# HGRN2 scores in 32-column tiles with compact copies, and two kinds of copy moved to ScalarE

## The chip, the cores and the metric

The kernel runs on one core of a Trainium2 chip. The metric is device time in microseconds (us) of one execution. The engines of the core are TensorE (PE in the profile, its weight loads PEld), VectorE (DVE), ScalarE (ACT), GpSimd (POOL) and SyncE (SP, which issues DMAs here). Each works through a queue of its own in order.

## The reference, cut to what matters

One decoder layer over 1024 positions: a projection of the normalised input, three groups of heads (HGRN2, a dilated window attention, RWKV-7), an output projection, a gated feed-forward part with a short convolution, a gated embedding and a last norm. The change is in the first two groups of heads. For one HGRN2 head, with 128 key and 128 value dimensions, f in (0, 1) and k = 1 - f:

```python
S_t = diag(f_t) S_{t-1} + (1 - f_t) i_t^T
o_t = S_t^T q_t
scores[i, j] = sum_k q[i, k] * (1 - f[j, k]) * prod(f[j+1 .. i, k])     # j <= i, in a chunk
o = scores @ i + (q * prod(f)) @ state
```

The attention computes, for four heads of 64 dimensions, softmax probabilities of a query block over its near and strided far keys, and multiplies them with the values.

## The kernel before, in words

The layer is a sequence of phases. The projections and RWKV-7 come first; the stretch that the change touches is the second part of the mixing phase (`phase_mix`), about 403 to 570 us in the profile; then come the output projection, the feed-forward part (Winograd-like products, lines L1523 and L1845) and the embedding gate. In the stretch of the change four streams of Python generators are taken in turn by `interleave`: A is HGRN2 head 0 and then head 2, B is head 1 and then head 3, C is the attention (`swa`), F is the rest of the input projection (`project_late`, tiles zp). The Tile framework schedules each engine's queue from this order, so a stream's wait delays the others that are queued behind it on the same engine.

**An HGRN2 head** (`hgrn_head`) holds its vectors with the key dimension on the partitions and 1024 positions along the free dimension, as two halves of 512 with four chunks of 128 positions each; one of the halves is stored in reversed order. Its tiles are f (zl), q (zl), the keys k (hk), the decayed queries qt, the scores S (hS, two halves `S3[0]`, `S3[1]`) and the products of f over growing blocks (hT). It first makes f and the keys 1 - f on VectorE (L1094) and qt = q * f (L1096). Then it makes the scores of each position with itself, two groups of four products 128x128x128 (L1112), and copies the diagonal out of PSUM with `copy_predicated` under a mask (L1114). Then come seven levels l with block size n = 2^(l-1) (1 to 64). A level has the keys of every second block in a compact order (ks, a ScalarE copy at L1123), multiplies them with the queries of the neighbouring block (four products 128x128x128, L1138), updates the keys (GpSimd or VectorE, L1140) and the queries (VectorE, L1142) for the next level, and copies from the 128x512 result those scores that the mask of the level marks (L1145). At level l only pairs of positions in neighbouring blocks of n are kept, so at n up to 16 all kept scores lie in 32x32 blocks on the diagonal of a chunk. After level 7, `triangles` moves one triangle into the other half (L1127). The rest of the head transposes values and keys, forms states and outputs (L1163 to L1237). A level's products wait for the queries of the level before (VectorE) and for ks (ScalarE), which waits for hk.

**The attention** makes, for each of eight query blocks of two head pairs, scores (tiles swq; far keys in products with 64 rows and 32 columns of the array, near keys with 64 rows and 128 columns), probabilities (lg), and in `swa_turn` transposes them (swt) and copies them from PSUM to SBUF (pT): for one head of the pair by ScalarE, for the other by VectorE (L1361). The values product reads pT later (swo).

`group` issues a list of products so that they stand together in TensorE's queue. All PSUM tiles of these streams but swq come from one pool of four banks (tag mx).

Of the kernel before, what the change touches and what calls it, by code (L numbers as in the profile page):

```python
# [10 lines left out]
F32 = mybir.dt.float32  # L11
F32R = mybir.dt.float32r
U8 = mybir.dt.uint8
AF = mybir.ActivationFunctionType
ALU = mybir.AluOpType
# [3 lines left out]
P = 128  # L19
T = 1024  # L20
HT = 512
# [16 lines left out]
CC_ID, CC_BONE, CC_MSK, CC_Q, CC_HG, CC_RU = 0, 128, 256, 512, 640, 640 + 9 * 128  # L38
NC0 = 640
# [3 lines left out]
def shape_constants():  # L43
    c = np.zeros((P, NCC), np.float32)
    pp = np.arange(P)[:, None]
    ff = np.arange(P)[None, :]
    c[:, CC_ID:CC_ID + P] = pp == ff
    same = (pp // 64) == (ff // 64)
    c[:, CC_BONE:CC_BONE + P] = same
    c[:, CC_MSK:CC_MSK + P] = same & (pp < ff)  # L50
    c[:, CC_MSK + P:CC_MSK + 2 * P] = same & (pp <= ff)
    c[:, CC_HG:CC_HG + P] = pp == ff
    for l in range(7):
        n = 1 << l
        c[:, CC_HG + (l + 1) * P:CC_HG + (l + 2) * P] = (pp // n) ^ 1 == ff // n
    c[:, CC_HG + 8 * P:CC_HG + 9 * P] = pp < ff
    c[:, CC_Q:CC_Q + P] = pp // 32 == ff // 32
    c[:, CC_RU:CC_RU + P] = same & (ff % 64 >= 32) & (pp % 64 < 32)
    qi, qr = pp % 32, pp // 32
    near = P + 4 * qi + qr - np.arange(2 * P)[None, :]  # L60

    def far(ds):
        return np.concatenate([P * d + 4 * (qi - np.arange(32)[None, :]) for d in ds], axis=1)

    d = np.concatenate([far((6, 5, 4, 3, 2)), np.full((P, 32), -1), near, far((7, 6, 5, 4, 3, 2)), near], axis=1)
    cnt = ((d >= 0) & (d <= 128)).astype(np.float64)
    cnt += (d >= 0) & (d <= 512) & (d % 4 == 0)
    cnt += (d >= 0) & (d <= 2048) & (d % 16 == 0)
    sw = np.where(cnt > 0, 8.0 * np.log(np.maximum(cnt, 1.0)), -1e30).astype(np.float32)
    return c, sw  # L70
# [14 lines left out]
class Trunk:  # L85
# [212 lines left out]
    def hgmask(self, l):  # L298
        o = CC_HG - NC0 + l * P
        return self.cmask[:, o:o + P]  # L300


    def proj(self, j, hooks={}):
# [777 lines left out]
    def hgrn_head(self, h):  # L1081
        nc, mxp, par, spool = self.nc, self.mxp, self.par, self.spool
        j0 = 8 + 4 * h

        def view(t, off, *dims):
            return bass.AP(t.tensor, t.offset + off, [t.ap[0], *dims])

        f = self.zload(j0, self.slot)
        q = self.zload(j0 + 1, self.slot)
        yield  # L1090
        nc.vector.tensor_scalar(f, f, self.olb[:, h:h + 1], self.lb[:, h:h + 1], ALU.mult, ALU.add)
        k = self.slot("hk")
        for a, b in ((0, HT), (HT, 0)):
            nc.vector.tensor_scalar(k[:, a:a + HT], f[:, b:b + HT], -1.0, 1.0, ALU.mult, ALU.add)  # L1094
        qt = self.slot("qt")
        nc.vector.tensor_tensor(qt, q, f, ALU.mult)  # L1096
        yield
# [3 lines left out]
        S3 = [S[:, a:a + HT].rearrange("p (c i) -> p c i", i=P) for a in (0, HT)]  # L1101

        def mask(l):
            return self.hgmask(l).unsqueeze(1).broadcast_to([P, 4, P])

        Tt = self.slot("hT")
        off = 0
        Tc = f
        for i in (0, 1):
            sc = mxp.tile([P, 4, P], F32, tag="mx", name=self.nm("hsc"))  # L1110
            for c in range(4):
                nc.tensor.matmul(sc[:, c, :], k[:, (1 - i) * HT + c * P:(1 - i) * HT + (c + 1) * P],  # L1112
                                 q[:, i * HT + c * P:i * HT + (c + 1) * P], start=True, stop=True)
            nc.vector.copy_predicated(S3[i], mask(0), sc)  # L1114

        def blocks(l):
            n = 1 << (l - 1)
            return n, HT // n, ([HT + n, 2], [2 * n, 256 // n], [1, n])

        def keys(l):  # L1120
            n, nb, half = blocks(l)
            ks = spool.tile([P, HT], F32, tag="sqt", name=self.nm("ks"), bufs=2)
            nc.scalar.copy(view(ks, 0, [n, 2], [2 * n, nb // 2], [1, n]), view(k, 0, *half))  # L1123
            return ks

        def triangles():
            nc.vector.copy_predicated(S3[1], mask(8), S3[0])  # L1127
            nc.gpsimd.affine_select(S3[0], S3[0], [[0, 4], [-1, P]], base=0, channel_multiplier=1, compare_op=ALU.is_ge, fill=0.0)

        last = h == 3  # L1130
        ks = keys(1)
        yield
        for l in range(1, 8):
            n, nb, half = blocks(l)
            qq = view(qt, 0, *half)
            sc = mxp.tile([P, 4, P], F32, tag="mx", name=self.nm("hsc"))
            for c in range(4):
                nc.tensor.matmul(sc[:, c, :], ks[:, c * P:(c + 1) * P],  # L1138
                                 view(qt, c * P, [2 * n, 64 // n], [HT + n, 2], [1, n]), start=True, stop=True)
            (nc.gpsimd if l % 2 else nc.vector).tensor_tensor(  # L1140
                view(k, 0, *half), view(k, 0, *half), view(Tc, nb + 1, [-nb - 1, 2], [2, nb // 2], [0, n]), ALU.mult)
            nc.vector.tensor_tensor(qq, qq, view(Tc, 1, [nb - 1, 2], [2, nb // 2], [0, n]), ALU.mult)  # L1142
            if l < 7:
                ks = keys(l + 1)
            nc.vector.copy_predicated(S3[0], mask(l), sc)  # L1145
            Tn = Tt[:, off:off + nb]
            T3 = Tc.rearrange("p (b two) -> p b two", two=2)
            nc.vector.tensor_tensor(Tn, T3[:, :, 0], T3[:, :, 1], ALU.mult)
            Tc = Tn
            off += nb  # L1150
            if l == 7:
                vc = self.zload(j0 + 2, self.slot)
                if last:
                    triangles()
            yield
        if not last:
            triangles()

        V = self.slot("hV")
        for hf in (0, 1):  # L1160
            pt = mxp.tile([P, HT], F32, tag="mx", name=self.nm("vt"))
# [4 lines left out]
        for hf in (0, 1):  # L1166
            pt = mxp.tile([P, HT], F32, tag="mx", name=self.nm("vt"))
# [10 lines left out]
        for hf in (0, 1):  # L1178
# [6 lines left out]
            for c in range(4):  # L1185
# [3 lines left out]
                dst = st[:, (cc + 1) * P:(cc + 2) * P]  # L1189
# [7 lines left out]
        o, sq = self.slot("ho"), kt  # L1197
# [152 lines left out]
    def swa_turn(self, sp, d, qb, den, lgs):  # L1350
        nc, w = self.nc, 64 * (qb // 2)
        if qb % 2 == 0:
            d["pT"] = [sp.tile([P, 2, HT], F32, tag="pT", name=self.nm("pT"), bufs=3) for _ in lgs]
        else:
            self.uid += 2
        cols = [w + b * P for b in range(2 if qb else 1)] + [b * P for b in range((w + 64) // P)]
        for lg, t, copy in zip(lgs, d["pT"], (nc.scalar.copy, nc.vector.tensor_copy)):
            pt = self.mxp.tile([P, HT], F32, tag="mx", name=self.nm("swt"))
            for i, c in enumerate(cols):
                nc.tensor.transpose(pt[:, i * P:(i + 1) * P], lg[:, c:c + P], self.ident)  # L1360
            copy(t[:, qb % 2, :len(cols) * P], pt[:, :len(cols) * P])  # L1361
        return qb, den, d["pT"]

    def swa_values(self, sp, d, q0, den, pT):
# [698 lines left out]
def lay_out(inp):  # L2063
    f = {k: np.asarray(v) for k, v in inp.items()}

    def cols(v):
        return v.reshape(-1, P).T

    lora = np.concatenate([f["rwkv_w2"][0], f["rwkv_a2"][0]], axis=0)
    par = np.concatenate(  # L2070
        [cols(f["norm_mix_g"][0]), cols(f["norm_ffn_g"][0]), cols(f["norm_ple_g"][0]), cols(f["final_norm_g"]),
         cols(f["hgrn_lower_bounds"][0]), cols(f["hgrn_gnorm_g"][0]), cols(f["rwkv_mu"][0]),
         cols(f["rwkv_w0"][0]), cols(f["rwkv_a0"][0]), cols(f["rwkv_k_k"][0]), cols(f["rwkv_k_a"][0]),
         cols(f["rwkv_r_k"][0].reshape(-1)), cols(f["rwkv_ln_w"][0]), cols(f["rwkv_ln_b"][0]),
         cols(f["ffn_conv_w"][0].reshape(-1)), cols(f["ffn_conv_b"][0]), lora, f["rwkv_g2"][0]], axis=1)
    cst, swm = shape_constants()
    return {
        "xT": np.ascontiguousarray(f["x"][0].T).reshape(ND, P, T),
        "pT": np.ascontiguousarray(f["p"][0, 0].T).reshape(2, P, T),
        "w_in": col_blocks(f["w_in"][0], in_blocks()),  # L2080
        "w_out": col_blocks(f["w_out"][0], range(0, 1024, P)),
        "ffn_up": col_blocks(f["ffn_up"][0], range(0, 5632, P)),
        "ffn_down": np.ascontiguousarray(f["ffn_down"][0]).reshape(NFF, P, 1024),
        "ple_gate": col_blocks(f["ple_gate"][0], range(0, 1024, P)),
        "ple_proj": np.ascontiguousarray(f["ple_proj"][0]).reshape(2, P, 1024),
        "par": np.ascontiguousarray(par),
        "cst": cst,
        "swm": swm,
    }
# [17 lines left out]
```

## Time and profile before

| | us |
|---|---|
| median of three runs | 1410.86 (1410.41 to 1413.49) |
| the profiled execution's own time | 1411.64 |
| its span, first to last instruction | 1409.9 |
| TensorE busy | 1391.4 (99%) |
| VectorE busy | 1082.1 (77%) |
| ScalarE busy | 635.2 (45%) |
| GpSimd busy | 447.2 (32%) |

In the groups of the profile a row reads: line, engine, operation, out<-in by the program's names, the part of the array in use (rows*columns) for TensorE, out<-in sizes, number, then busy us, mean ns of one, and the engine's idle time just ahead of them with what ended it. In the timeline a row is a run of like instructions: start, us from the first's start to the last's end, engine, line, operation, number, and in brackets the idle time ahead of it. An fp32 product stands as two matmul instructions (two passes); the 32-bit "fp32r" products with 512 columns (zp, dp, bg, bv) stand as one. Matmuls overlap, so a matmul's own duration is longer than what it adds to TensorE's time; the step from start to start, or from end to end, is that.

### The profile page before, as it was taken

What the parts mean: (1) busy time and instruction counts of PE and PEld (TensorE: products, weight loads), DVE (VectorE), ACT (ScalarE), POOL (GpSimd) and SP (SyncE); (2) the same over time, 40 slices, a digit from 0 to 9 for tenths busy, and PEclk for the clock granted to TensorE, in tenths of its full rate; (3) what the DMA queues carried; (4) which work ended last, traced back from release to release, by engine and by line L of the source; (5) the groups of instructions that cost most, each with busy time, mean ns of one, the idle gap of its engine ahead of it and who ended that gap; (6) DMA issues with size and microseconds to landing.
All of it is one profiled execution on the core that took longest, in us unless ns stands there. A gap on an engine that the chain in (4) does not pass through costs nothing.

```text
span 1409.9 us, 20332 instructions
## 1 busy us (share of the span) xinstructions
PE 1391.4 (99%) x7458; PEld 1155.3 (82%) x7458; DVE 1082.1 (77%) x1671; ACT 635.2 (45%) x1193; POOL 447.2 (32%) x360
## 2 busy tenths in 40 slices
PE   9999999999999989999999999999999999999997
PEld 7888887888878878888888888888888888888886
DVE  7667575684776788457988888898888799777685
ACT  7531453213444666354544344443435444455552
POOL 2322442223432332221345454454543000002353
PEclk9999999999999999999999999999999999999998
DMA  5223022240252321573333232323334963351443
GB/s 214 79 87 116 31 76 60 67 135 31 76 193 66 107 83 46 172 261 135 121 112 111 86 101 98 110 100 112 112 98 137 358 229 103 113 159 53 129 150 133
DMA packets 80020, 167.78 MB, mean 119 GB/s; under 512 B 20081, under 2 KB 22257, under 8 KB 79921
## 3 DMA queue, kind: packets, MB, share of 16 engines
q1 hardware_dynamic: 66144, 145.97, 31.2%
q10 hardware_dynamic: 12832, 16.98, 3.6%
q0 software_dynamic: 944, 3.54, 0.7%
q8 instruction: 59, 0.97, 0.3%
q14 instruction: 41, 0.33, 0.1%
HBM read 120.05 MB, written 46.40 MB: 118 GB/s over the span
## 4 chain that ended last, share of the span: by engine, by line
PE 94%; DVE 3%; ACT 1%; DMA 1%; issue 1%; POOL 1%; SPq 0%; DVEq 0%; ACTq 0%; POOLq 0%
PE bg L1523 17%; PE bv L1523 13%; PE dp L135 9%; PE dp L137 9%; PE dp L139 9%; PE bg L1845 7%; PE bv L1845 7%; PE hsc L1138 2%; PE bv L135 1%; PE bv L139 1%; PE bv L137 1%; PE bg L139 1%; PE bg L137 1%; PE bg L135 1%; PE zp L135 1%; PE zp L139 1%
## 5 line engine op out<-in xcount | busy, mean ns | idle before, releaser
L135 PE MATMUL dp<-xh,whi 128*128 128x512 f32 x544 | 196.9, 407 | 0.8 <-ACT xh L397 0.8
L137 PE MATMUL dp<-xl,whi 128*128 128x512 f32 x544 | 188.3, 391 | 1.1 <-DVE xl L398 1.1
L139 PE MATMUL dp<-xh,wlo 128*128 128x512 f32 x544 | 188.9, 392 | 0.0
L113 POOL TENSOR_TENSOR wlo<-wraw,whi 128x512 fp32r<-128x512 f32 x63 | 89.2, 1420 | 243.1 <-ACT whi L111 239.0
L113 POOL TENSOR_TENSOR wlo<-raw,whi 128x512 fp32r<-128x512 f32 x84 | 135.7, 1634 | 74.1 <-ACT whi L111 74.1
L1523 PE MATMUL bg<-t,whi 128*128 128x512 f32 x352 | 132.4, 389 | 0.0
L111 ACT CAST whi<-wraw 128x512 fp32r<-128x512 f32 x120 | 72.7, 617 | 117.8 <-PE dp L137 74.9
L139 PEld LDWEIGHTS dp<-xh,wlo 128*128 128x128 f32 x544 | 102.1, 188 | 22.0 <-issue 0.5
L135 PEld LDWEIGHTS dp<-xh,whi 128*128 128x128 f32 x544 | 101.3, 188 | 22.4 <-issue 3.0
L137 PEld LDWEIGHTS dp<-xl,whi 128*128 128x128 f32 x544 | 102.4, 188 | 20.9 <-DVE xl L398 1.7
L113 POOL TENSOR_TENSOR wlo<-s,whi 128x512 fp32r<-128x512 f32 x44 | 66.0, 1500 | 161.5 <-ACT whi L111 150.5
L1845 PE MATMUL bg<-t,whi 128*128 128x512 f32 x308 | 94.9, 389 | 0.0
L1845 PE MATMUL bv<-t,whi 128*128 128x512 f32 x308 | 94.9, 389 | 0.0
L111 ACT CAST whi<-s 128x512 fp32r<-128x512 f32 x66 | 39.0, 620 | 123.3 <-PE bg L1523 115.2
L111 ACT CAST whi<-raw 128x512 fp32r<-128x512 f32 x88 | 52.6, 619 | 92.0 <-issue 48.8
L180 POOL TENSOR_TENSOR rst<-rst,mhalf 128x4 f32<-128x4 f32 (+1 forms) x9 | 10.2, 1138 | 219.8 <-DVE rst L178 219.8
L1523 PEld LDWEIGHTS bg<-t,whi 128*128 128x128 f32 x352 | 66.0, 188 | 13.7
L1841 ACT CAST t<-t 128x512 fp32r<-128x512 f32 x77 | 47.8, 622 | 46.6 <-PE bv L1845 28.8
L1845 PEld LDWEIGHTS bv<-t,whi 128*128 128x128 f32 x308 | 57.8, 188 | 12.0
L1845 PEld LDWEIGHTS bg<-t,whi 128*128 128x128 f32 x308 | 57.8, 188 | 11.9
L1523 PE MATMUL bg<-t,wlo 128*128 128x512 f32 x176 | 67.2, 389 | 0.0
L113 DVE TENSOR_TENSOR wlo<-wraw,whi 128x512 fp32r<-128x512 f32 x57 | 43.5, 766 | 30.5 <-ACT whi L111 26.6
(455 smaller groups left out, 3561.9 us busy)
## 6 DMA issues: line engine op xcount, KB each, us to landing
raw<-in_ffn_up_dram SPq DMA_DIRECT2D x44, 512.0 KB, 3.7
wraw<-in_w_in_dram SPq DMA_DIRECT2D x29, 512.0 KB, 3.7
z<-zst SPq DMA_DIRECT2D x18, 512.0 KB, 2.8
gb<-ct SPq DMA_DIRECT2D x33, 256.0 KB, 2.2
t<-gb SPq DMA_DIRECT2D x33, 256.0 KB, 2.8
t<-gt SPq DMA_DIRECT2D x33, 256.0 KB, 2.7
zl<-z SPq DMA_DIRECT2D x16, 512.0 KB, 4.8
wraw<-in_ple_gate_dram SPq DMA_DIRECT2D x16, 512.0 KB, 3.5
```

The costliest lines, as they stand in the source:

```text
L111: nc.scalar.copy(hi, src)
L113: eng.tensor_tensor(lo, src, hi.bitcast(F32), ALU.subtract)
L135: nc.tensor.matmul(ps[hf], wh, xh[hf], start=first, stop=False)
L137: nc.tensor.matmul(ps[hf], wh, xl[hf], start=False, stop=False)
L139: nc.tensor.matmul(ps[hf], wl, xh[hf], start=False, stop=last)
L180: nc.gpsimd.tensor_tensor(r2[:, :n], r[:, :n], self.mhalf[:, :n], ALU.pow)
L1138: nc.tensor.matmul(sc[:, c, :], ks[:, c * P:(c + 1) * P], view(qt, c * P, [2 * n, 64 // n], [HT + n, 2], [1, n]), start=True, stop=True)
L1523: nc.tensor.matmul(ps, w[part == 2][:, s], X[k][part == 1], start=start and k == part == 0, stop=k == 3 and part == 2, skip_group_check=no ...
L1841: nc.scalar.copy(xh, x)
L1845: nc.tensor.matmul(ps[m], wt[part == 2][:, m * P:(m + 1) * P], (xh, xl)[part == 1], start=k == part == 0, stop=k == NK - 1 and part == 2)
```

## The change

1. The scores of a position with itself and of levels 1 to 6 (n up to 32) are made in products of 32 key columns and 32 queries, those of level 7 in products of 32 key columns and 64 queries. A product (chunk c, block b) writes partitions 32b to 32b+31 of the result. A group has 16 products (32 for the first, which now holds both halves in one PSUM tile), all with the full 128 rows and 32 columns of the array. They are issued through `group`.
2. The result of a group is 128x128 (128x256 for the first and for level 7). For levels 1 to 5 a `copy_predicated` of 128x128 gathers them in a new SBUF tile D (hD, first filled by a plain copy). At level 6, D and the level's result are spread into S by two `copy_predicated` of 128x512 (`place`), at level 7 one; one more puts the second half's diagonal in place.
3. The keys 1 - f are made by ScalarE (activation Copy with scale and bias) instead of VectorE.
4. All transposed probabilities pT are copied by ScalarE.
5. The constant masks are laid out anew to match, in the same space and with the same loads.

```diff
@@ hgrn_head
         for a, b in ((0, HT), (HT, 0)):
-            nc.vector.tensor_scalar(k[:, a:a + HT], f[:, b:b + HT], -1.0, 1.0, ALU.mult, ALU.add)
+            nc.scalar.activation(k[:, a:a + HT], f[:, b:b + HT], AF.Copy, scale=-1.0, bias=1.0)
...
+        def place(i, l, src):
+            w = src.shape[2]
+            dst, m = (t.rearrange("p c (b i) -> p c b i", i=w) for t in (S3[i], mask(l)))
+            nc.vector.copy_predicated(dst, m, src.unsqueeze(2).broadcast_to([P, 4, P // w, w]))
+
+        blocks32 = [(c, b, c * P + 32 * b) for c in range(4) for b in range(4)]
+        D = self.sp.tile([P, 4, 32], F32, tag="hD", name=self.nm("hD"), bufs=2)
...
-        for i in (0, 1):
-            sc = mxp.tile([P, 4, P], F32, tag="mx", name=self.nm("hsc"))
-            for c in range(4):
-                nc.tensor.matmul(sc[:, c, :], k[:, (1 - i) * HT + c * P:(1 - i) * HT + (c + 1) * P],
-                                 q[:, i * HT + c * P:i * HT + (c + 1) * P], start=True, stop=True)
-            nc.vector.copy_predicated(S3[i], mask(0), sc)
+        sc = mxp.tile([P, 2, 4, 32], F32, tag="mx", name=self.nm("hsc"))
+        self.group([(sc[32 * b:32 * b + 32, i, c], k[:, (1 - i) * HT + o:(1 - i) * HT + o + 32], q[:, i * HT + o:i * HT + o + 32])
+                    for i in (0, 1) for c, b, o in blocks32])
+        nc.vector.tensor_copy(D, sc[:, 0])
+        place(1, 0, sc[:, 1])
...
-            sc = mxp.tile([P, 4, P], F32, tag="mx", name=self.nm("hsc"))
-            for c in range(4):
-                nc.tensor.matmul(sc[:, c, :], ks[:, c * P:(c + 1) * P],
-                                 view(qt, c * P, [2 * n, 64 // n], [HT + n, 2], [1, n]), start=True, stop=True)
+            sc = mxp.tile([P, 4, max(32, n)], F32, tag="mx", name=self.nm("hsc"))
+
+            def queries(b, o):
+                if n < 32:
+                    return view(qt, o, [2 * n, 16 // n], [HT + n, 2], [1, n])
+                e = 32 * b // n ^ 1
+                return view(qt, o - 32 * b + e // 2 * 2 * n + e % 2 * (HT + n), [1, n])
+
+            self.group([(sc[32 * b:32 * b + 32, c], ks[:, o:o + 32], queries(b, o)) for c, b, o in blocks32])
...
-            nc.vector.copy_predicated(S3[0], mask(l), sc)
+            if l < 6:
+                nc.vector.copy_predicated(D, self.hgnear(l), sc)
+            else:
+                place(0, l - 4, sc)
+            if l == 6:
+                place(0, 1, D)
@@ swa_turn
-        for lg, t, copy in zip(lgs, d["pT"], (nc.scalar.copy, nc.vector.tensor_copy)):
+        for lg, t in zip(lgs, d["pT"]):
...
-            copy(t[:, qb % 2, :len(cols) * P], pt[:, :len(cols) * P])
+            nc.scalar.copy(t[:, qb % 2, :len(cols) * P], pt[:, :len(cols) * P])
```

The queues as built show how the instructions move. SyncE's queue is the same; GpSimd's has the same operations. On TensorE, levels 4 and 5 of head 1 stand between outputs of head 0 (hpo), the attention's transposes (swt) and the projection (zp). Before:

```order
L1217 MATMUL hpo_4364<-hst_4237,qt_3742 128x128
L1138 MATMUL hsc_4373<-qt_3996,ks_4261 128x128 x4
L1360 MATMUL swt_4384<-cst,lg_4305 128x128 x4
L1360 MATMUL swt_4390<-cst,lg_4308 128x128 x4
L1138 MATMUL hsc_4408<-qt_3996,ks_4380 128x128 x4
L135 MATMUL zp_4431<-xh_105,whi_4421 128x512
```

and now:

```order
L1238 MATMUL hpo_4533<-hst_4394,qt_3742 128x128
L1340 MATMUL hsc_4542<-qt_4080,ks_4430 32x32 x16
L1381 MATMUL swt_4565<-cst,lg_4474 128x128 x4
L1381 MATMUL swt_4571<-cst,lg_4477 128x128 x4
L1340 MATMUL hsc_4589<-qt_4080,ks_4561 32x32 x16
L136 MATMUL zp_4624<-xh_105,whi_4614 128x512
```

Nothing has moved there but the products themselves: 16 small ones where 4 full ones stood, with full-array products on both sides (a size is partitions x columns of the result). Counted over the whole queue, products that follow one with another part of the array (rows*columns) in use number 96 before and 137 now.

On VectorE, where head 2 is at its levels 4 and 5 and head 3 begins (xl belongs to the output of head 1), there stood:

```order
L1142 TENSOR_TENSOR qt_4577<-qt_4577,hT_4609 128x2x32x8
L1145 COPY_PREDICATED hS_4607<-cmask,hsc_4870 128x512
L1237 SCALAR_TENSOR_TENSOR zl_4807<-vt_4881,par,zl_4807 128x512
L1237 SCALAR_TENSOR_TENSOR zl_4807<-vt_4887,par,zl_4807 128x512
L1094 TENSOR_SCALAR hk_4941<-zl_4897 128x512
L1361 COPY pT_4859<-swt_4924 128x384
L162 TENSOR_TENSOR xl_4660<-zl_4807,xh_4659 128x512
L1142 TENSOR_TENSOR qt_4577<-qt_4577,hT_4609 128x2x16x16
L1145 COPY_PREDICATED hS_4607<-cmask,hsc_4929 128x512
```

and now:

```order
L1158 TENSOR_TENSOR qt_4795<-qt_4795,hT_4828 128x2x32x8
L1162 COPY_PREDICATED hD_4827<-cmask,hsc_5148 128x128
L1258 SCALAR_TENSOR_TENSOR zl_5073<-vt_5171,par,zl_5073 128x512
L1364 ISA lg_5206,sden_5191<-swq_5192,swmask 128x384
L1364 ISA sden_5191 128x1
L1258 SCALAR_TENSOR_TENSOR zl_5073<-vt_5177,par,zl_5073 128x512
L1096 TENSOR_SCALAR zl_5187<-zl_5187,olb,lb 128x1024
L1158 TENSOR_TENSOR qt_4795<-qt_4795,hT_4828 128x2x16x16
L163 TENSOR_TENSOR xl_4902<-zl_5073,xh_4901 128x512
L1162 COPY_PREDICATED hD_4827<-cmask,hsc_5219 128x128
```

Between the two updates of qt the keys hk and the copy pT have left the queue, an attention score (lg) and the f of head 3 (zl, L1096) have come in, and xl stands behind the second update instead of ahead of it.

More of the change, by code (lines that the diff above doesn't have):

```diff
@@ L51, in shape_constants @@
     c[:, CC_MSK + P:CC_MSK + 2 * P] = same & (pp <= ff)
[L52 to L56, printed above, removed]
+    wide = pp == ff, pp // 32 == ff // 32, (pp // 32) ^ 1 == ff // 32, (pp // 64) ^ 1 == ff // 64, pp < ff
+    for i, m in enumerate(wide):
+        c[:, CC_HG + i * P:CC_HG + (i + 1) * P] = m
+    for l in range(5):
+        n, o = 1 << l, CC_HG + 5 * P + 32 * l
+        c[:, o:o + 32] = (pp % 32 // n) ^ 1 == ff[:, :32] // n
     c[:, CC_Q:CC_Q + P] = pp // 32 == ff // 32
@@ L300, in hgmask, with hgnear @@
         return self.cmask[:, o:o + P]
+    def hgnear(self, l):
+        o = CC_HG - NC0 + 5 * P + (l - 1) * 32
+        return self.cmask[:, o:o + 32].unsqueeze(1).broadcast_to([P, 4, 32])
     def proj(self, j, hooks={}):
@@ L1126, in triangles @@
         def triangles():
-            nc.vector.copy_predicated(S3[1], mask(8), S3[0])
+            nc.vector.copy_predicated(S3[1], mask(4), S3[0])
             nc.gpsimd.affine_select(S3[0], S3[0], [[0, 4], [-1, P]], base=0, channel_multiplier=1, compare_op=ALU.is_ge, fill=0.0)
```

## The prediction

> **What bounds the kernel now.** I read the page's busy times and chain first, then the busy times of the stretch that the change touches, then what TensorE waits for in it. From the page:
>
> ```profile
> PE 1391.4 (99%) x7458; PEld 1155.3 (82%) x7458; DVE 1082.1 (77%) x1671; ACT 635.2 (45%) x1193; POOL 447.2 (32%) x360
> ...
> PE 94%; DVE 3%; ACT 1%; DMA 1%; issue 1%; POOL 1%; SPq 0%; DVEq 0%; ACTq 0%; POOLq 0%
> ```
>
> TensorE is busy 99% of the span and is 94% of the chain that ended last. The stretch of HGRN2 and the attention by the windows view (its length, then the busy us of TensorE, the weight loads, VectorE, ScalarE and GpSimd, then the granted clock), and TensorE's waits in it:
>
> ```profile
> 403.00:570.00 167.00, 161.65 (x1364) 134.57 (x1363) 131.42 (x286) 96.25 (x252) 49.20 (x43) 0.99 0.25 86
> ...
> PE hsc L1138 <- DVE qt L1142: 2.1, 1, 2.1
> PE vt L1303 <- ACT sV L1296: 1.0, 1, 1.0
> PE swt L1360 <- DVE zst L530: 0.6, 1, 0.6
> ```
>
> Here too TensorE is the bound (161.65 of 167 us, so 5.35 us idle), ahead of VectorE (131.42) and ScalarE (96.25). The longest wait, 2.1 us for qt, has an aftermath:
>
> ```profile
> 524.00:526.00 2.00, 2.00 (x11) 2.00 (x11) 2.00 (x4) 0.00 (x0) 0.00 (x0) 0.50 0.00 0
> 523.67 2.07 PE L1138 MATMUL hsc<-qt,ks 128*128 128x128 f32 x8 [2.10 <-DVE qt L1142]
> ```
>
> The granted clock was 0.50 in these 2 us, and a group of eight passes took 2.07 us where others take 1.06 (below). Idle time and this slow patch together, say 7 us, are what waits cost in the stretch today. So the time follows TensorE's work; later phases are TensorE's as well and start when this one ends, so I carry a gain in the stretch to the end in full.
>
> **What the products cost today.** What counts is the step from a group's start to its follower's. The counts, then the first group (two halves, 16 passes), a level with n of 4 or more, one with n = 2 and one with n = 1, each with its follower:
>
> ```profile
> L1138 PE MATMUL hsc<-qt,ks x224: 272/275/580, 416.7 to 560.5; 128*128 128x128 f32 x112
> ...
> L1112 PE MATMUL hsc<-zl,hk x64: 270/275/421, 412.8 to 527.9; 128*128 128x128 f32 x64
> ...
> 412.76 1.95 PE L1112 MATMUL hsc<-zl,hk 128*128 128x128 f32 x16
> 414.54 0.27 PE L1360 MATMUL swt<-cst,lg 128*128 128x128 f32 x1
> ...
> 471.83 1.06 PE L1138 MATMUL hsc<-qt,ks 128*128 128x128 f32 x8
> 472.72 1.04 PE L1360 MATMUL swt<-cst,lg 128*128 128x128 f32 x8
> ...
> 457.08 1.13 PE L1138 MATMUL hsc<-qt,ks 128*128 128x128 f32 x8
> 458.04 1.72 PE L1184 MATMUL hkv<-hV,hkt 128*128 128x128 f32 x14
> ...
> 504.99 1.58 PE L1138 MATMUL hsc<-qt,ks 128*128 128x128 f32 x8 [0.58 <-DVE hst L1193]
> 506.39 0.39 PE L1215 MATMUL hpo<-hV,hS 128*128 128x128 f32 x2
> ```
>
> That is 1.78, 0.89, 0.96 and 1.40 us (queries that lie singly in memory, n = 1, stream slower). Per head 1.78 + 1.40 + 0.96 + 5 x 0.89 = 8.59 us, for four heads 34.4 us of TensorE time, all on the path.
>
> **What they will cost.** There will be 4 x 32 + 24 x 16 + 4 x 16 = 576 products, so 1152 passes where 288 were. No row shows 128 rows with 32 columns of the array. The nearest rows are RWKV-7's products with 128 rows and 64 columns, two tiles of the array side by side, and the attention's with 64 rows and 32 columns, eight tiles:
>
> ```profile
> 152.82 1.05 PE L1001 MATMUL pgm<-pb,X 128*128 128x128 f32 x8
> 153.80 0.69 PE L1014 MATMUL pn<-XV,W 128*64 128x64 f32 x16
> 154.32 0.64 PE L1020 MATMUL pyo<-XV,W 128*64 128x64 f32 x16
> 154.88 0.50 PE L135 MATMUL dp<-xh,whi 128*128 128x512 f32 x1
> 155.22 0.40 PE L137 MATMUL dp<-xl,whi 128*128 128x512 f32 x1
> 155.46 0.40 PE L139 MATMUL dp<-xh,wlo 128*128 128x512 f32 x1
> ...
> 406.14 0.44 PE L1319 MATMUL swq<-zl,zl 64*32 64x64 f32 x16
> ```
>
> In pn, 16 passes take 0.69 us of which the last one's own 0.22: with about 0.03 per pass, two tiles at once, one tile takes a pass of 64 columns each 0.058 us. In swq eight tiles do two passes each in 0.44 us, of which 0.29 are one pass's latency and 0.10 each tile's step to its second pass; its keys lie four elements apart, so this is the dear end. A pass of 32 columns is then 0.029 us (half of pn's) to 0.052 (half of swq's) per tile, four tiles at once. I take 0.029: pn has all 128 rows and operands without gaps, like most groups here. In units of 32 columns, four heads have per tile 24 groups of 8 passes, 4 first groups of 16 and 4 of level 7 with 8 passes of twice the columns: 320 x 0.029 = 9.3 us, up to 16.6; n = 1 adds some 0.5 (1.40 against 0.89). I use 10 us, with ends 9.3 and 17.1.
>
> **What stands between them.** The array's part in use changes 96 times before and 137 times now (counted in the queue). Each change shows as a gap between ends. pgm ends at 153.87, 16 pn passes end at 154.49: 0.62 where 16 x 0.029 = 0.46 would do, 0.16 more. pyo ends at 154.96, the dp product at 155.38: 0.42, where the step of such products is 0.24 (155.22 to 155.46): 0.18 more. And for score products after swq:
>
> ```profile
> 429.56 0.70 PE L1319 MATMUL swq<-zl,zl 64*128 64x256 f32 x4
> 430.19 1.16 PE L1138 MATMUL hsc<-qt,ks 128*128 128x128 f32 x8
> ```
>
> swq ends at 430.26, the group at 431.35: 1.09 against 0.89, 0.20 more. So 41 more changes cost 41 x 0.18 = 7.4 us (6.6 to 8.2). The Trainium skill speaks against the change here: "TensorEngine Tiling (Array Packing)", Key Properties, says that a change of the tiling mode drains TensorE. The trace agrees and gives the price, the 0.16 to 0.20 us above. TensorE's net is -34.4 + 10 + 7.4 = -17.0 us, with ends -18.5 and -9.1.
>
> **The other engines.** They lie beside TensorE's work; what they add or lose counts only by queueing. Rows for VectorE and ScalarE:
>
> ```profile
> L1145 DVE COPY_PREDICATED hS<-cmask,hsc 128x512 f32<-128x512 uint8 x28 | 20.5, 733 | 0.0
> L1193 DVE SCALAR_TENSOR_TENSOR hst<-hst,hT,hkv 128x128 f32<-128x128 f32 x24 | 8.2, 342 | 0.3
> L1114 DVE COPY_PREDICATED hS<-cmask,hsc 128x512 f32<-128x512 uint8 x8 | 5.7, 740 | 1.4 <-PE hsc L1112 1.3
> L1094 DVE TENSOR_SCALAR hk<-zl 128x512 f32<-128x512 f32 x8 | 3.4, 453 | 0.1
> ...
> L1123 ACT COPY ks<-hk 128x512 f32<-128x512 f32 x28 | 17.6, 631 | 19.2 <-DVE hk L1140 8.8 <-PE hsc L1138 5.2 <-POOL hk L1140 5.1
> ...
> L1361 ACT COPY pT<-swt x16: 265/476/586, 414.9 to 551.9; 128x384 f32<-128x384 f32 x8, 128x512 f32<-128x512 f32 x4, 128x128 f32<-128x128 f32 x2, 128x256 f32<-128x256 f32 x2
> L1361 DVE COPY pT<-swt x16: 280/553/690, 416.5 to 552.7; 128x384 f32<-128x384 f32 x8, 128x512 f32<-128x512 f32 x4, 128x128 f32<-128x128 f32 x2, 128x256 f32<-128x256 f32 x2
> ```
>
> VectorE loses 36 copies of 0.73 (26.2 us), the keys (3.4) and 16 pT (8.8), and gets 16 copies of 128x512 (11.7) and 24 of 128x128, at the 0.34 of the nearest row 8.2: -18.5 us. ScalarE gets 8 key halves at the 0.63 of ks (5.0) and 16 pT (7.6): +12.6 us. If the stretch becomes 150 us, VectorE is busy for 113 of it (75%, from 79%), ScalarE for 109 (73%, from 58%).
>
> What this does to the 7 us of waits is the choice that no row settles. VectorE's queue, behind which the 2.1 us wait stood, gets shorter by hk and pT just there: all of that stall and its slow patch may go (-4). ScalarE's ks, for which the next level's products wait, now stands behind two pT copies (0.95 us) and, at a head's start, two key halves (1.3 us); with four heads and sixteen pairs of copies some will be felt, and TensorE's work, the cover of all this, is a tenth shorter (+6 at worst). I take +2.
>
> Sum: 1411.6 - 17 + 2 = 1396.6 us for an execution like the profiled one, whose span of 1409.9 has 1.7 around it. The median of the runs lies 0.8 lower: **1396 us**. Its own ends: -18.5 - 4 gives 1388, -9.1 + 6 gives 1408.
>
> **Rivals.** First, the levels' chain takes over. From ks (0.63) over products, qt and hk, level follows level through four queues. After 480 us only heads 1 to 3 and the attention are left to interleave, and the waits of 2.1 and 1.0 us are there. If the pace there stays, only the products ahead of 480 pay:
>
> ```profile
> L1138 PE MATMUL hsc<-qt,ks x96: 272/275/424, 416.7 to 474.6; 128*128 128x128 f32 x96
> L1112 PE MATMUL hsc<-zl,hk x32: 270/275/275, 412.8 to 442.4; 128*128 128x128 f32 x32
> ```
>
> 128 of 288 passes, 0.44 x 17 = 7.5 us: 1403 us. For it: VectorE's 79% and ScalarE's rise. Against: the stretch after 480 still has projection and output products (zp, dp) queued as cover, and VectorE is relieved. If the waits took all of the 17 us, the time would be 1411.
>
> Second, and slower: starts set the pace, not columns. If every pass costs what a pn pass does, (0.69 - 0.22)/16 = 0.029 us, however narrow and whichever tile it uses, 1152 passes cost 33.4 us and with the changes 40.8, 6.4 more than the 34.4 of today; with +2 of waits 1419 us. It decides from (34.4 - 7.4 - 2)/1152 = 0.022 us per pass on. Against it: in the swq row 16 passes fit in 0.44 us with 0.29 of latency, so 15 starts in 0.15, 0.010 each. The Trainium skill has such a floor: "TensorE: Matmul & The Clock Gate", Part 1, says that start-to-start never drops below about 25 ns. By that figure, as an estimate, 28.8 us and the changes come to 36.2, and the time to about 1415; the swq row speaks against it where tiles alternate.
>
> **How the numbers follow.** Forecast 0.75, first rival 0.13, all eaten by waits 0.05, second rival 0.07. The range of 1389 to 1407 leaves out the second rival, the eaten gain and the tips of the forecast. A difference of 0.2% (2.8 us) is about what a measurement can tell from none. Faster by more: the forecast and the first rival, but for a tip, 0.87; within it 0.05; slower 0.08.
>
> **What would show it.** Right: groups of 16 products ending about 0.4 us after what precedes them (0.23 of passes, 0.16 of change), followed by a gap of 0.18 to 0.20; TensorE's busy time near 1375 us; 128x128 copies near 0.34 us; idle time in the stretch below 8 us. Wrong: passes of one group starting 0.02 us apart or more, changes dearer than 0.3 us, or TensorE waiting for ks or pT from ScalarE over 5 us in all.

## The result, and the profile after

The changed kernel takes 1402.29 us (median of six runs, 1401.35 to 1404.04), the kernel before 1412.41 us beside it (six runs, 1410.41 to 1413.49): a ratio of 0.9931, 95% interval 0.9918 to 0.9944. It is faster by 10 us where 15 were forecast. The profiled execution took 1402.43 us, with a span of 1400.7 (before: 1409.9). The page's busy times, after:

```profile
PE 1375.6 (98%) x8322; PEld 1134.4 (81%) x8322; DVE 1071.1 (76%) x1651; ACT 643.7 (46%) x1217; POOL 450.1 (32%) x360
```

TensorE's busy time fell by 15.8 us, the span only by 9.2: part of the shorter work turned into waiting. The windows view says where. Its columns are window and length, busy us of TensorE, weight loads, VectorE, ScalarE and GpSimd, then the granted clock. Before, in two parts of the stretch:

```profile
403.00:480.00 77.00, 76.07 (x589) 62.18 (x588) 57.58 (x127) 41.86 (x102) 18.68 (x17) 1.00 0.37 124
480.00:570.00 90.00, 85.58 (x777) 72.39 (x776) 73.84 (x160) 54.38 (x150) 30.53 (x27) 0.98 0.16 54
```

After, the same parts and the whole stretch:

```profile
403.00:480.00 77.00, 73.36 (x1063) 56.19 (x1061) 52.13 (x118) 49.21 (x120) 19.55 (x17) 1.00 0.37 128
480.00:570.00 90.00, 81.53 (x1211) 64.23 (x1212) 70.99 (x162) 58.06 (x167) 34.14 (x28) 0.96 0.20 67
...
403.00:570.00 167.00, 154.89 (x2274) 120.42 (x2273) 123.11 (x279) 107.28 (x286) 53.69 (x45) 0.98 0.28 95
```

Idle time of TensorE is the length less its busy time: 0.93 became 3.64 ahead of 480 us and 4.42 became 8.47 behind it, in all 5.35 became 12.11. The clock column fell too, from 0.99 to 0.98: there are two spells of 3.4 us at half clock instead of one. Whether the second spell belongs to the kernel or to this one execution is open: the mean granted clock of the six runs lies between 0.994 and 0.996, and three of them have the 0.996 of the profiled execution before.

The products themselves, in TensorE's timeline after (start, us to the last one's end, engine, line, operation, number): the first group, n = 1, and two levels of n of 4 or more with their followers, and one more group with what precedes it:

```profile
413.48 0.76 PE L1340 MATMUL hsc<-zl,hk 128*32 128x32 f32 x64
414.17 0.44 PE L1381 MATMUL swt<-cst,lg 128*128 128x128 f32 x2
414.54 0.54 PE L1340 MATMUL hsc<-qt,ks 128*32 128x32 f32 x32
415.01 1.07 PE L1340 MATMUL swq<-zl,zl 64*32 64x64 f32 x20
...
468.50 0.46 PE L1340 MATMUL hsc<-qt,ks 128*32 128x32 f32 x32
468.89 1.09 PE L1381 MATMUL swt<-cst,lg 128*128 128x128 f32 x8
469.92 0.46 PE L1340 MATMUL hsc<-qt,ks 128*32 128x32 f32 x32
470.31 0.50 PE L136 MATMUL zp<-xh,whi 128*128 128x512 f32 x1
470.64 0.40 PE L138 MATMUL zp<-xl,whi 128*128 128x512 f32 x1
```

From a group's start to its follower's start, 1.78 us became 0.69, 1.40 became 0.47 and 0.89 became 0.39. End to end: swt ends at 469.98, the group at 470.38, 0.40 later; the zp behind it ends at 470.81 and the next at 471.04, steps of 0.43 and 0.23, so the change back costs 0.20. A level costs 0.60 us where it cost 0.89.

What TensorE waits for in the stretch, after (us in all, times, longest):

```profile
PE hsc L1340 <- ACT ks L1134: 2.7, 3, 1.6
PE vt L1190 <- DVE ob L1422: 2.3, 1, 2.3
PE swq L1340 <- DVE sden L1364: 1.2, 1, 1.2
PE hsc L1340 <- DVE hD L1162: 1.1, 1, 1.1
PE hsc L1340 <- DVE ob L1411: 0.6, 1, 0.6
PE swt L1381 <- DVE hS L1114: 0.6, 1, 0.6
```

Before, one wait of 2.1 us on qt led. Now the waits are many, on VectorE more than on ScalarE, and about half of the time in these lines is for work of the attention (ob and sden). The longest is not for data: vt is a head's keys, transposed, while the instruction on ob reads swd, and by the code vt and swd lie in the same pool of four PSUM banks. So it is, as far as the code tells, a wait for a free bank; a pool with more banks wasn't run. The same wait in VectorE's timeline, with GpSimd's rows of the same time:

```profile
485.25 1.77 DVE L163 TENSOR_TENSOR xl<-oc,xh 128x512 fp32r<-128x512 f32 x1
486.95 1.12 DVE L163 TENSOR_TENSOR xl<-zl,xh 128x512 fp32r<-128x512 f32 x1
487.99 1.75 DVE L163 TENSOR_TENSOR xl<-ob,xh 128x512 fp32r<-128x512 f32 x1
489.67 0.69 DVE L318 TENSOR_TENSOR zp<-zp,rstd 128x512 f32<-128x512 f32 x1
490.27 0.67 DVE L1422 TENSOR_TENSOR ob<-ob,swd 128x512 f32<-128x512 f32 x1
...
484.67 1.81 POOL L114 TENSOR_TENSOR wlo<-wraw,whi 128x512 fp32r<-128x512 f32 x1 [0.51 <-ACT whi L112]
487.50 3.38 POOL L163 TENSOR_TENSOR xl<-oc,xh 128x512 fp32r<-128x512 f32 x2
```

TensorE starts again at 491.08, after 2.33 us. VectorE had no gap: it worked off three xl first. TensorE's queue held no other ready work ahead of vt. And the three xl took 4.64 us where an xl with no GpSimd instruction beside it takes 0.67 to 0.69 in all the traces here, 2.0 to 2.1 for three. By these numbers, as an estimate, the lengthening of some 2.6 us is as long as the whole wait.

The copies after, by groups, with the update of qt ahead of them; the last row is of the tile view, which gives the shortest, the median and the longest in ns:

```profile
L1158 DVE TENSOR_TENSOR qt<-qt,hT 128x512 f32<-128x512 f32 x24 | 21.2, 884 | 1.4 <-PE hsc L1340 1.4
L1114 DVE COPY_PREDICATED hS<-cmask,hsc 128x512 f32<-128x512 uint8 x12 | 8.8, 734 | 0.5 <-POOL hS L1105 0.5
L1162 DVE COPY_PREDICATED hD<-cmask,hsc 128x128 f32<-128x128 uint8 x20 | 5.9, 293 | 0.0
L1114 DVE COPY_PREDICATED hS<-cmask,hD 128x512 f32<-128x512 uint8 x4 | 4.5, 1115 | 0.0
L1124 DVE COPY hD<-hsc 128x128 f32<-128x128 f32 x4 | 1.1, 282 | 1.3 <-PE hsc L1340 1.3
...
L1114 DVE COPY_PREDICATED hS<-cmask,hD x4: 748/1170/1372, 437.6 to 548.2; 128x512 f32<-128x512 uint8 x4
```

and the update of qt before:

```profile
L1142 DVE TENSOR_TENSOR qt<-qt,hT 128x512 f32<-128x512 f32 x24 | 17.6, 731 | 6.8 <-PE hsc L1138 6.7
```

The small copies are cheaper than forecast (293 and 282 ns against 0.34 us), and the four that spread D are dearer on the mean (1115 ns against 0.73 us). Together they come to 20.3 us where 19.9 were forecast. The mean of the four hides two kinds: the one that ran with no GpSimd instruction beside it took 748 ns, about the forecast's figure, and the three that overlapped with one took 1129 to 1372. The update of qt, which every level's products need, did the same: 24 of them take 21.2 us where they took 17.6.

### The profile page after: what moved, and what is told of

The parts are those of the page before. It is cut to its first block, busy times and chain, and to the rows that moved or that the text cites. A ratio compares the mean times of both kernels' runs of the same rounds, so it can differ in the third digit from the quotient of the medians.

```text
span 1400.7 us, 22064 instructions
## 1 busy us (share of the span) xinstructions
PE 1375.6 (98%) x8322; PEld 1134.4 (81%) x8322; DVE 1071.1 (76%) x1651; ACT 643.7 (46%) x1217; POOL 450.1 (32%) x360
## 4 chain that ended last, share of the span: by engine, by line
PE 58%; DVE 5%; ACT 1%; issue 1%; POOL 0%; DVEq 0%; ACTq 0%; POOLq 0%
PE bg L1544 16%; PE bv L1544 12%; PE bg L1866 7%; PE bv L1866 7%; PE dp L140 2%; PE dp L136 2%; PE dp L138 2%; PE bv L136 1%; PE bv L140 1%; PE bv L138 1%; PE bg L136 1%; PE bg L140 1%; PE bg L138 1%; ACT hkt L1226 0%; DVE xl L163 0%
```

## The experiments

The theory to test: TensorE's work shrank as forecast, and its shorter work no longer covers the chains through the other queues, so that part of the gain comes back as waits. The rivals: the copies moved to ScalarE delay ks and with it the products; the compact copies cost or gain; or the order that the scheduler happened to choose decides.

A table first, since all runs read alike. The median and the ratio are of all runs of a kernel, the ratio against the kernel before that ran beside it (medians 1413.05 us beside 1 to 4, 1412.42 beside 5 to 8, 1412.50 beside 9 to 11). So a difference between medians of different groups can be off by about 0.6 us. Span, idle and slow are of the one profiled execution. Idle is 167 us less TensorE's busy time between 403 and 570 us; slow is the time at half clock in the clock record there. Kernels 5, 7 and 11 have another 3.4 us of it near the program's start, outside the stretch.

| kernel | median, us | ratio (95% interval) | span | idle | slow | span less idle |
|---|---|---|---|---|---|---|
| before | 1412.41 | | 1409.9 | 5.35 | 3.4 | 1404.6 |
| after | 1402.29 | 0.9931 (0.9918–0.9944) | 1400.7 | 12.11 | 6.8 | 1388.6 |
| 1 ScalarE moves undone | 1401.44 | 0.9920 (0.9904–0.9936) | 1398.4 | 11.09 | 3.4 | 1387.3 |
| 2 ScalarE moves alone | 1414.67 | 1.0011 (1.0002–1.0019) | 1412.2 | 6.50 | 6.8 | 1405.7 |
| 3 same tile in a row | 1409.82 | 0.9977 (0.9968–0.9986) | 1406.2 | 5.35 | 0 | 1400.9 |
| 4 projection later | 1398.85 | 0.9897 (0.9884–0.9910) | 1396.4 | 9.30 | 3.4 | 1387.1 |
| 5 wide copies | 1398.92 | 0.9901 (0.9884–0.9918) | 1397.5 | 10.61 | 3.4 | 1386.9 |
| 6 copies left out (not the whole result) | 1395.92 | 0.9881 (0.9867–0.9896) | 1393.5 | 8.66 | 0 | 1384.8 |
| 7 projection a little later | 1399.30 | 0.9902 (0.9884–0.9920) | 1397.4 | 9.40 | 3.4 | 1388.0 |
| 8 1 and 4 together | 1400.25 | 0.9913 (0.9898–0.9928) | 1397.8 | 11.19 | 3.4 | 1386.6 |
| 9 before, projection later | 1413.66 | 1.0004 (0.9996–1.0013) | 1410.2 | 5.55 | 3.4 | 1404.7 |
| 10 5 and 4 together | 1396.61 | 0.9881 (0.9866–0.9896) | 1396.1 | 8.71 | 3.4 | 1387.4 |
| 11 small products alone | 1404.39 | 0.9939 (0.9925–0.9953) | 1403.8 | 12.60 | 10.2 | 1391.2 |

**1. The ScalarE moves undone.** The changed kernel with keys and every second pT back on VectorE:

```diff
-            nc.scalar.activation(k[:, a:a + HT], f[:, b:b + HT], AF.Copy, scale=-1.0, bias=1.0)
+            nc.vector.tensor_scalar(k[:, a:a + HT], f[:, b:b + HT], -1.0, 1.0, ALU.mult, ALU.add)
...
-        for lg, t in zip(lgs, d["pT"]):
+        for lg, t, copy in zip(lgs, d["pT"], (nc.scalar.copy, nc.vector.tensor_copy)):
...
-            nc.scalar.copy(t[:, qb % 2, :len(cols) * P], pt[:, :len(cols) * P])
+            copy(t[:, qb % 2, :len(cols) * P], pt[:, :len(cols) * P])
```

> The changed kernel with the keys 1 - f and every second pT copy back on VectorE (the small products and compact copies alone). If the added waits of the changed kernel come from ScalarE's 12.6 us more of work: some 5 us of the 8 lost go, about 1397 us. If they come from TensorE's shorter time as cover, with VectorE busy for 12 us more: 1402 to 1406 us, idle time of TensorE in the stretch 11 us or more.

Measured: 1401.44 us, not to be told from the changed kernel, and just under the range given for cover. The stretch:

```profile
403.00:570.00 167.00, 155.91 (x2284) 121.44 (x2283) 131.09 (x304) 97.79 (x262) 56.81 (x45) 0.99 0.28 98
```

ScalarE has 9.5 us less to do there than in the changed kernel and TensorE still waits for 11.09 us. ScalarE's added load alone is not what makes the waits. VectorE has 8.0 us more to do here, so the run trades one load for the other.

**2. The ScalarE moves alone.** The same lines changed the other way in the kernel before.

> The kernel before with the keys and all pT copies on ScalarE, its full-array products kept. If ScalarE's queue makes the waits: about 5 us over before, 1417 us. If the cover decides: within 2 us of before, 1410 to 1414 us.

Measured: 1414.67 us, slower by 1.6 (0.3 to 2.7, from the interval) than the kernel before beside it: within the 2 us expected if cover decides, far from the 5 us expected of ScalarE's queue. VectorE's relief bought nothing. The longest wait of before is still there, and longer:

```profile
PE hsc L1138 <- DVE qt L1142: 3.7, 1, 3.7
```

The forecast gave up to 4 us for this stall going once hk and pT left VectorE's queue. With them gone it grew from 2.1 to 3.7. In the changed kernel itself no wait on qt is in the list; others stand in its place.

**3. The same tile in a row.** The changed kernel with a group's products ordered by column tile, so that a tile gets its eight passes one after the other:

```diff
-        blocks32 = [(c, b, c * P + 32 * b) for c in range(4) for b in range(4)]
+        blocks32 = [(c, b, c * P + 32 * b) for b in range(4) for c in range(4)]
```

> The changed kernel with the 16 products of a group in another order: the four products of one column tile follow each other. If the tiles of the array work side by side and a tile takes a pass each 0.029 us, a group's 32 passes need 0.93 us in place of 0.24: with 10 us of passes as they are that is up to 28 us more, some of it in place of waits, 1420 to 1430 us. If starts set the pace whichever tile they use (the second rival): no change, 1402 us.

Measured: 1409.82 us. A level and its follower in TensorE's timeline, then the stretch:

```profile
458.86 0.90 PE L1340 MATMUL hsc<-qt,ks 128*32 128x32 f32 x32
459.68 0.50 PE L136 MATMUL zp<-xh,whi 128*128 128x512 f32 x1
```

```profile
403.00:570.00 167.00, 161.65 (x2250) 130.42 (x2249) 119.96 (x277) 106.31 (x285) 50.67 (x44) 1.00 0.26 88
```

A level takes 0.82 us where it took 0.39, with the same instructions: the tiles do work side by side when they alternate. The row of a group less one pass's 0.20, over 31 steps, gives (0.46 - 0.20)/31 = 0.008 us per pass alternating and (0.90 - 0.20)/31 = 0.023 in a row. The expected time missed on two counts. The added work is smaller than the 28 us reckoned with: TensorE's busy time is 1387.2 us against 1375.6, of which the two half-clock spells hold some 3.4, so about 15 us. And the waits answered: with those 15 us more of work TensorE's idle time fell from 12.11 to 5.35 us, what it was before the change, and the half-clock spells vanished. Slower TensorE work covers the waits. That is the theory's central claim, seen in the opposite direction. Nor can the order of the queues be the reason here: over the whole trace the instructions of VectorE, ScalarE and GpSimd come in the same order as in the changed kernel's, and TensorE's groups too.

**4. The projection later.** The changed kernel with the turns of stream F, whose zp products stand ready for TensorE, moved to where the levels of heads 2 and 3 run:

```diff
-    LATE = 0, 1, 4, 7, 9, 11, 13, 15, 17
+    LATE = 0, 1, 4, 7, 10, 14, 18, 22, 26
```

> The changed kernel with the last projections (zp) spread to rounds up to 26 of the interleaving, where they end at 17 now. If the waits come from too little other work for TensorE late in the stretch: 3 to 5 us less, 1397 to 1399 us, idle time of TensorE in the stretch under 9 us. If they come from ScalarE's added work: within 1.5 us of the changed kernel, 1401 to 1404 us.

Measured: 1398.85 us, 3.4 faster than the changed kernel. The stretch:

```profile
403.00:570.00 167.00, 157.70 (x2294) 123.27 (x2293) 122.30 (x280) 112.71 (x293) 52.49 (x45) 0.99 0.29 102
```

Idle time fell from 12.11 to 9.30 and one half-clock spell went. The time is in the range expected if cover was lacking, the idle time a little above its 9 us. This edit moves the order of the queues too, so kernel 9 has to tell cover from order.

**5. Wide copies.** The changed kernel, with all small products, but a 128x512 copy at every level with the masks of before, and no D:

```diff
-        nc.vector.tensor_copy(D, sc[:, 0])
+        place(0, 0, sc[:, 0])
         place(1, 0, sc[:, 1])
...
-            if l < 6:
-                nc.vector.copy_predicated(D, self.hgnear(l), sc)
-            else:
-                place(0, l - 4, sc)
-            if l == 6:
-                place(0, 1, D)
+            place(0, l, sc)
```

> The changed kernel with its small products, but every level's result spread into S by a 128x512 copy (masks as before, no D): VectorE gets 24 wide copies for 24 compact ones and loses the four that spread D, 7.5 us more of work. If VectorE's queue makes the waits: 4 to 7 us more, 1406 to 1409 us. If the compact copies lie beside TensorE's work: within 1.5 us of the changed kernel, 1401 to 1404.

Measured: 1398.92 us, 3.4 faster than the changed kernel. Neither expectation had it. Its copies by groups, then the stretch:

```profile
L1113 DVE COPY_PREDICATED hS<-cmask,hsc 128x512 f32<-128x512 uint8 x36 | 25.9, 733 | 1.5 <-POOL hS L1104 1.3 <-PE hsc L1334 0.2
```

```profile
403.00:570.00 167.00, 156.39 (x2289) 122.26 (x2289) 128.62 (x276) 107.12 (x286) 53.33 (x45) 0.99 0.28 99
```

VectorE is busy for 5.5 us more there, and TensorE waits for 1.5 us less. So the compact copies gain nothing here: their saving lies beside TensorE's work. Whether they cost something (the long spreading copies stand in VectorE's queue at level 6), or the scheduler's other order is the better one by chance, this run doesn't say, since the built order of the queues differs around the levels.

**6. Copies left out.** The changed kernel with only the copies of level 7 and the triangles left, so that the other scores are missing from its result; GpSimd clears both halves of S instead of one:

```diff
-        nc.gpsimd.memset(S[:, HT:], 0.0)
+        nc.gpsimd.memset(S, 0.0)
...
-        nc.vector.tensor_copy(D, sc[:, 0])
-        place(1, 0, sc[:, 1])
...
-            if l < 6:
-                nc.vector.copy_predicated(D, self.hgnear(l), sc)
-            else:
+            if l == 7:
                 place(0, l - 4, sc)
-            if l == 6:
-                place(0, 1, D)
```

> The changed kernel without the copies of scores but the one of level 7 (the scores of the other levels and the diagonals are left out of the result; GpSimd clears both halves of S): VectorE loses 16 us of work. If VectorE's queue makes the waits: 4 to 7 us less, 1395 to 1398 us, idle time of TensorE in the stretch under 8 us. If the levels' chain over ScalarE and GpSimd makes them: within 1.5 us, 1401 to 1404.

Measured: 1395.92 us.

```profile
403.00:570.00 167.00, 158.34 (x2304) 124.53 (x2303) 111.90 (x245) 108.77 (x291) 57.28 (x47) 1.00 0.30 106
```

That is 6.4 us under the changed kernel, in the range that was expected if VectorE's queue makes the waits, though the idle time of 8.66 us isn't under the expected 8. Against kernel 5, which has 16.7 us more for VectorE in the stretch (128.62 against 111.90), it is only 3.0 us. So the copies are a link of the chains that TensorE waits for, worth 3 to 6 us with most of them gone, but not the whole: 8.66 us is still 3.3 above the idle time before.

**7. The projection a little later.** As 4, with `LATE = 0, 1, 4, 7, 9, 13, 17, 21, 25`.

> The changed kernel with the last projections in rounds 0, 1, 4, 7, 9, 13, 17, 21, 25: the early ones as now, the late ones spread. If the cover decides: 4 to 6 us less than the changed kernel, 1396 to 1398 us, since the early waits of the wider spread do not come. If spreading gained by chance of order alone: 1399 to 1403 us.

Measured: 1399.30 us, 3.0 faster than the changed kernel: short of what was expected for cover, and just inside the range given for an order that gains by chance (1399 to 1403). By itself it doesn't decide between the two. That two placements give nearly the same speaks against one lucky order.

**8. 1 and 4 together**: the moves to ScalarE undone, and the later projection.

> The small products and compact copies with the keys and every second pT copy back on VectorE, and the projections spread to round 26. If the ScalarE moves are worth nothing either way: 1397 to 1400 us, as with the same spread and the moves. If they help once there is cover: 2 us or more slower than that, over 1401 us.

Measured: 1400.25 us, between the two expectations and 1.4 slower than kernel 4. The runs overlap (1399.49 to 1402.4, and 1396.99 to 1400.52), so whether the moves are worth anything beside the later projection stays open.

**9. The kernel before, with the projection later.** The edit of 4 in the kernel before.

> The kernel before, with its full 128x128 products, and only the turns of the projection's parts moved later (0, 1, 4, 7, 10, 14, 18, 22, 26). It tells whether the 3 us that the same move gave to the changed kernel are cover for its waits, or a better order that any kernel would take. Theory (cover): before, TensorE is idle for only 5.7 us of the stretch, so there is little to win: 1410 to 1414, ratio 0.998 to 1.001. Rival (the order is simply better): 1408 to 1410, ratio 0.9975 or below.

Measured: 1413.66 us, a ratio of 1.0004 (0.9996 to 1.0013).

```profile
403.00:570.00 167.00, 161.45 (x1366) 134.02 (x1365) 137.20 (x291) 101.86 (x264) 50.50 (x43) 0.99 0.25 88
```

The move that gives the changed kernel 3.4 us gives the old one nothing: its idle time is 5.55 us, where it was 5.35 before (not 5.7, as the expectation has it). The later projection isn't a better order as such. It paid only where TensorE lacked cover.

**10. Wide copies and the projection later**: 5 and 4 together.

> Small products, wide copies (128x512 with the masks of before, no tile D), keys and all pT on ScalarE, and the projection's parts at 0, 1, 4, 7, 10, 14, 18, 22, 26. If the wide copies' queue order and the later projection each remove waits of their own, it comes to 1395 to 1397 (1398.9 less 2 to 3.4). If both only cover the same 2 to 3 us of waits, it stays at 1398 to 1400.

Measured: 1396.61 us, ratio 0.9881 (0.9866 to 0.9896), the fastest kernel of the study that does the whole computation: 5.7 us under the changed kernel. That is where it was expected if each edit removes waits of its own, though the intervals of 4, 5 and 10 overlap.

**11. The small products alone**: kernel 5 with the edit of 1, so that nothing of the change is left but the products.

> Small products with the wide copies, and the keys and every second pT back on VectorE: the products are the only part of the change that is left. Theory (the products bring all of it, the copies and the moves to ScalarE nothing): 1398 to 1402, as with the wide copies (1398.9) and with the moves undone (1401.4). If VectorE's load does matter once both of its reliefs are gone (24 copies at 0.73 instead of 0.29, 3.4 us of keys and 8.8 of pT more): 1404 to 1409, its busy time becoming the levels' pace.

Measured: 1404.39 us (1401.79 to 1407.59). The longest of its waits:

```profile
PE hsc L1334 <- DVE hk L1098: 2.4, 1, 2.4
```

This is slower than kernel 5 by 5.5 us, and than kernel 1 by 3 with intervals that overlap; it lies in the range expected if VectorE's load matters. Here the first products of a head wait for the keys (hk) in VectorE's queue. So VectorE's load seems to matter once it has neither relief. With either one (1 or 5) the kernel takes 1399 to 1401.5, and with both (the changed kernel) no less. Which part of these few microseconds is load and which is order stays open: the three runs differ in both.

## Why the prediction was right, and where it was off

**The sign, and TensorE's term, were right.** The last column of the table takes the waits out. Among kernels with one half-clock spell in the stretch it is 1404.6 and 1404.7 with the old products (before, 9) and 1386.6 to 1388.0, mean 1387.2, with the small ones (1, 4, 5, 7, 8, 10): -17.4 us, where the term said -17.0. Its parts hold too. A level was forecast at 8 x 0.029 for its passes and 0.18 for each change of the array's part, 0.59 us with both changes; it took 0.60. TensorE's busy time is 1375.6 where about 1375 was to be seen. One slip in the working is small: between the 16 passes of pn lie 15 steps, so its row gives 0.031 us and not 0.029 per pass, some 0.7 us more in the sum. That a gain in the stretch is carried to the end in full held too: 9.9 us at the stretch's end (rows below), 9.2 in the span.

**The second rival, that starts set the pace, is out.** It needed 0.022 us per pass; passes on alternating tiles come 0.008 apart. Experiment 3 shows that it is the alternation that does it. The Trainium skill's "TensorE: Matmul & The Clock Gate", Part 1, puts a floor of about 25 ns under the step between starts; passes on one tile, at 23 ns, come near it, and alternating tiles go far below. The Trainium skill's "TensorEngine Tiling (Array Packing)", Key Properties, says that different tiles work in parallel, and experiment 3 agrees.

**The step that failed is the size of the waits: "I take +2", with ends of -4 and +6.** Idle time rose by 12.11 - 5.35 = 6.8 us, and a second half-clock spell came (1388.6 against the mean of 1387.2, some 1.4 us): +8.2 in place of +2, and beyond the dear end. With -17.4 that gives the -9.2 of the spans. The second spell may be the draw of this execution, but the idle time by itself (6.8) is already beyond the dear end. The prediction named the right cause among others, "TensorE's work, the cover of all this, is a tenth shorter", and priced it too low. The total still fell inside the range because TensorE's term came as forecast and used up none of its own dear end. Idle "below 8 us" was to show it right; it was 12.1.

**What the waits are was half right.** The step blamed ks behind pT and keys in ScalarE's queue. One wait of that kind is there, ahead of the products at 516.72, in ScalarE's timeline:

```profile
514.70 0.62 ACT L1366 ACTIVATE lg<-lg,sden 128x384 f32<-128x384 f32 x1
515.22 0.19 ACT L1366 ACTIVATION_READ_ACCUMULATOR lg<-lg,sden 128x1 f32 x1
515.31 0.84 ACT L1382 COPY pT<-swt 128x384 f32<-128x384 f32 x2
516.04 0.63 ACT L1134 COPY ks<-hk 128x512 f32<-128x512 f32 x1
```

Two pT stand ahead of ks, and TensorE waits for 1.60 us. But ks and pT come to about 3.5 us in all, under the 5 that would have put the blame there, and without the moves (experiment 1) the idle time is 11.09. So the moves mostly decide which wait shows; cover decides more of how much is waited. Experiments 3, 4 and 9 show that: more TensorE work removes the added waits with the queues in the same order, ready work placed later removes a part, and the same placement does nothing where the work is longer. How the waiting is shared out among the chains, the copies (experiment 6), the banks and the instructions that GpSimd lengthens, stays open.

**The first rival** (1403 us, the levels' chain takes over) comes nearer in time than the forecast's number. But it put the whole gain ahead of 480 us and left the pace behind it as it was. The same two groups of TensorE's queue, before and then after, say otherwise:

```profile
491.64 0.60 PE L198 MATMUL swd<-cst,par 128*128 128x128 f32 x4
571.61 0.38 PE L1236 MATMUL vt<-cst,ho 128*128 128x128 f32 x2
...
486.72 0.60 PE L199 MATMUL swd<-cst,par 128*128 128x128 f32 x4
561.71 0.38 PE L1257 MATMUL vt<-cst,ho 128*128 128x128 f32 x2
```

The lead is 4.9 us at the first and 9.9 at the second: half of the gain came behind 480. The new waiting is spread the same way, 2.7 us ahead of 480 and 4.1 behind it. And the chain isn't the levels' alone; the attention's ob and sden are in it as well.

**VectorE's -18.5 us and ScalarE's +12.6** were rightly kept out of the sum, but VectorE's relief came out smaller: its busy time fell by 11.0 us (1082.1 to 1071.1). The copies, the keys and pT gave about what was forecast; instructions that the change doesn't touch got longer, the updates of qt by 3.6 us, and two kinds of xl by some 2.7 us. The prediction had no term for that. That the stall on qt would go just because hk and pT leave VectorE's queue was wrong (experiment 2).

## What to carry to other kernels

When a kernel's bound engine gets shorter work, take the idle time that it will have as a term of its own: the other engines' chains do not shrink, and here 8 of 17 us came back as waits and slow clock. Look for ready work of the bound engine that can be placed later, since that is cheap (one line gave 3.4 us here) and pays only after such a change. Relief for an engine off the bound is worth trying one piece at a time: here the compact copies or the ScalarE moves were enough (kernels 1 and 5), and the two together were slower than the moves with wide copies. And read the rows of the engine that gets relief again afterwards: here instructions that nobody touched grew longer beside GpSimd, and took back some 7 of VectorE's 18 us.

## What the runs showed of the hardware

- fp32 passes of 32 columns with 128 rows come 0.008 us apart when four column tiles alternate, and 0.023 us when one tile gets eight passes in a row.
- Spells of 3.4 us at half of TensorE's granted clock followed short waits. After the waits of 1.60 and 1.18 us that end at 516.72 and 518.35, the clock of the changed kernel reads

```profile
519.00:521.00 2.00, 2.00 (x61) 1.17 (x57) 2.00 (x4) 1.10 (x4) 0.18 (x1) 0.50 0.04 8
```

  and the other spell begins at 491.4, after the wait of 2.33. Not every such wait was followed by one: in kernel 5 a wait of 2.80 us that ends at 514.68 had no spell, and one of 2.46 that ends at 520.36 had one. The Trainium skill's "TensorE: Matmul & The Clock Gate", Part 1, speaks of an idle window of about 3.4 us; the spell's length agrees, and the waits ahead of the spells were shorter here. In the table's last column, small-product kernels with one spell in the stretch stand at 1387.2 on the mean, the changed kernel with two at 1388.6, and kernel 11 with three, and a fourth at its start, at 1391.2: 1.3 to 1.4 us a spell, beside the wait itself, where half of 3.4 would be 1.7. How many spells an execution has varies for one and the same kernel: of the 47 runs of the kernel before beside the experiments, the 11 with a mean granted clock of 0.997 took 1411.0 us on the mean, and the 9 with 0.993 took 1414.8.
- A `copy_predicated` of 128x512 from PSUM took 0.73 us on the mean, and one of 128x128 from PSUM 0.293.
- VectorE instructions whose operands all lie in SBUF can take twice as long while GpSimd works. Over the six kernels with the tile D, the copy that spreads it took 0.72 to 0.75 us in the 6 cases with no GpSimd instruction beside it, and 0.76 to 1.63 in the other 18. Over all 13 traces the update of qt took 0.65 to 0.70 us in 173 such cases and up to 2.13 in the other 139, many of which were not slowed. The copies of 128x512 scores from PSUM stayed at 0.69 to 0.80 us either way.
